# Seven products instead of plain sums for the second pair of weight chunks, in three of seven groups of an MLP, with block sums prepared during the attention part

## The chip, the cores and the metric

One core of a Trainium2 chip. The time is that of the program on the device in microseconds (us); the time before is the median of 3 runs. All engines of the core run their own instruction streams in order: TensorE (PE; its weight loads are listed as PEld), VectorE (DVE), ScalarE (ACT), GpSimd (POOL) and SyncE (SP), which here only issues DMAs. Differences of less than 0.2% (2.3 us) are not told apart.

## The reference

One decoder layer for 256 tokens of width 2048, in float32: three groups of mixers, an output projection, and an MLP of width 8192.

```python
def token_mixers(xn, ...):
    proj = jnp.einsum('bsd,de->bse', xn, w_in)
    # A: sparse attention; a small indexer scores all keys, the top 64 of each query are kept
    # B: mLSTM, chunkwise; C: differential attention
    ...
    return jnp.concatenate([y_a, y_m, y_c], axis=-1)

def reference(x, ...):
    mixed = token_mixers(x, ...)
    x = layer_norm(ALPHA * x + mixed @ w_out, ln1_g, ln1_b)
    h = jnp.square(jax.nn.relu(x @ w_up))
    return layer_norm(ALPHA * x + h @ w_down, ln2_g, ln2_b)
```

## The kernel before

**Splitting.** Every float32 operand of TensorE is used as a sum hi + lo of two rounded parts. A weight block [128 x 1024] comes as half of a 1 MB load (`load_raw`, L86, on SP's queue, three `raw` buffers), ScalarE casts it to hi (L90) and VectorE subtracts, lo = raw - hi (L91). Four buffers hold hi and four hold lo. TensorE needs three kinds of matmuls in a product, hi x hi, hi x lo and lo x hi.

**Units.** `unit_t` (L158, L159) computes 128 columns of a projection from one load of 1 MB: two halves of eight pairs of matmuls, 512 and 256 columns each. After each half `tick()` moves a clock on and runs work that was put off for so many ticks. `run_units` (L208 to L210) does the same for value projections. In mixer A the indexer's top 64 are found on VectorE by eight rounds of MAX8 and MATCH_REPLACE8 (L261, L262) on two blocks of queries, masked on GpSimd by AFFINE_SELECT (L264), between the splits of the units that run on TensorE meanwhile.

**MLP.** The hidden layer is cut into eight groups of eight units. While the units of group g + 1 are computed (`up`), group g is multiplied with its part of `w_down`, whose 2048 columns are four chunks of 512. Chunks 0 and 1 together are a matrix of 2 x 2 blocks and are done by the seven products of Strassen's scheme in Winograd's form (`product`, L884 to L886, 12 matmuls each): `pair_steps` makes the four needed sums of weight blocks on VectorE (L910 to L921, [128 x 2048] each) between the products. `make_blocks` and `make_sums` (L846, L853) prepare the same on the side of h in the tile `ms`, whose slices by form are `forms`. Chunks 2 and 3 are done plainly (`plain`, 48 matmuls each, L958 to L960). A string gives the order: U is a unit, a the next product of chunks 0 and 1, c and d the plain chunks. `out_block` and `macc` are where results add up; four of chunk pair 0's products stay in PSUM over all groups, the other three are added to `acc` by VectorE (L899). `pair_sums` joins the products at the end. A scheduler orders each engine's stream beforehand.

Of the kernel before, what the change touches and what calls it, by code (L numbers as in the profile page):

```python
# [11 lines left out]
F32 = mybir.dt.float32  # L12
# [12 lines left out]
FG = 8  # L25
FT = DFF // P // FG
TOPK = 64
ALPHA = 2.0 ** 0.25
EPS = 1e-5
LAM_INIT = 0.8 - 0.6 * math.exp(0.0)  # L30
# [12 lines left out]

def slopes(n):
    return [float(np.float32(2.0) ** np.float32(-8.0 * i / n)) for i in range(1, n + 1)]


@with_exitstack
def trunk_kernel(ctx: ExitStack, tc: tile.TileContext, xT, x, w_qi, w_t, w_va0, w_va, w_vm0, w_vm, w_vc,
# [21 lines left out]
    def tick():  # L71
        clock[0] += 1
        due = [f for d, f in queue if d <= clock[0]]
        queue[:] = [(d, f) for d, f in queue if d > clock[0]]
        for f in due:
            f()


    raws = [wp] * 3
# [22 lines left out]


    xs = fix.tile([P, KT, 2 * S], F32R, name="xs")
    ms = fix.tile([P, KT, 2 * S], F32R, name="ms")

    rx = fix.tile([P, 4240], F32, name="rx")

    ry = fix.tile([P, 4656], F32, name="ry")


    ones = mp.tile([P, P], F32, name="ones")
# [411 lines left out]
    for h in range(HM):  # L524
# [2 lines left out]
        m_head(h, q, k)  # L527
        conv_silu(13 + 2 * h, HM + h, k)


    sl_c = slopes(HC)
    sc_c = 64 ** -0.5
# [297 lines left out]

    A11, A12, A21, A22, S1, S2, S3, S4 = range(8)
    HT = FT // 2
    forms = ms.rearrange("p a b -> p (a b)").rearrange("p (f s k t) -> p f s k t", f=8, s=2, k=HT)

    macc = ry[:, 0:4 * 512].rearrange("p (i n) -> p i n", i=4)
    KEPT = {1: 0, 5: 1, 6: 2, 7: 3}
# [25 lines left out]
    def load_blocks(g, p):  # L862
        b11, b22, b21 = (fp.tile([P, 2048], F32, tag=n, name=n, bufs=1) for n in ("b11", "b22", "b21"))
        b12 = ry[:, 2048:4096]
        nc.sync.dma_start(b11, w_down[g, 2 * p, 0])
        nc.sync.dma_start(b12, w_down[g, 2 * p + 1, 0])
        nc.sync.dma_start(b22, w_down[g, 2 * p + 1, 1])
        nc.sync.dma_start(b21, w_down[g, 2 * p, 1])
        return b11, b12, b22, b21

    def product(g, p, i, f, b):

        if p == 0 and i in KEPT:
            if g == 0:
                kept[i] = mx("pk")
            ps, first, last = kept[i], g == 0, g == FG - 2
        else:
            ps, first, last = psb.tile([P, 512], F32, tag="big", name="pp"), True, True
        for q in range(2):
            hi, lo = split(b, 1024 * q, 1024 * q + 1024)  # L880
            for kk in range(2):
                k = 2 * q + kk
                w_hi, w_lo = hi[:, 512 * kk:512 * kk + 512], lo[:, 512 * kk:512 * kk + 512]
                nc.tensor.matmul(ps, forms[:, f, 0, k, :], w_hi, start=first and k == 0, stop=False)  # L884
                nc.tensor.matmul(ps, forms[:, f, 0, k, :], w_lo, start=False, stop=False)  # L885
                nc.tensor.matmul(ps, forms[:, f, 1, k, :], w_hi, start=False, stop=last and k == HT - 1)  # L886
        if p == 0 and i in KEPT:
            return
        if i in KEPT:
            a = macc[:, KEPT[i]]  # L890
            if g == 0:
                nc.scalar.copy(a, ps)
                return
        else:
            a = out_block(p, *((0, 0), (0, 1), (1, 0))[i - 2])
            if g == 0:
                nc.vector.scalar_tensor_tensor(a, a, ALPHA, ps, ALU.mult, ALU.add)
                return
        nc.vector.tensor_add(a, a, ps)  # L899

    def out_block(p, t, c):
        return acc[:, t, 1024 * p + 512 * c:1024 * p + 512 * c + 512]
# [1 line left out]
    def pair_steps(g, p, blocks):  # L904

        b11, b12, b22, b21 = blocks
        product(g, p, 1, A11, b11)
        yield
        product(g, p, 2, A12, b21)
        nc.vector.tensor_sub(b12, b12, b11)  # L910
        yield
        product(g, p, 3, S4, b22)
        nc.vector.tensor_sub(b22, b22, b12)
        yield
        product(g, p, 6, S2, b22)
        yield
        product(g, p, 5, S1, b12)
        nc.vector.tensor_sub(b11, b22, b11)
        yield
        product(g, p, 7, S3, b11)  # L920
        nc.vector.tensor_sub(b21, b21, b22)  # L921
        yield
        product(g, p, 4, A22, b21)
        yield

    def pair_sums(p):

        m = macc
        if p == 0:
            raw = wp.tile([P, 2048], F32, tag="raw", name="raw", bufs=3)  # L930
            m = raw.rearrange("p (i n) -> p i n", i=4)
            for i, j in KEPT.items():
                nc.scalar.copy(m[:, j], kept[i])
        p1, p5, p6, p7 = (m[:, j] for j in range(4))
        (c11, c12), (c21, c22) = ([out_block(p, t, c) for c in range(2)] for t in range(2))
        nc.vector.tensor_add(p6, p6, p1)
        nc.vector.tensor_add(p7, p7, p6)
        nc.vector.tensor_add(p6, p6, p5)
        nc.vector.tensor_add(p5, p5, p7)
        nc.vector.tensor_add(c11, c11, p1)  # L940
        nc.vector.tensor_add(c12, c12, p6)
        nc.vector.tensor_add(c21, c21, p7)
        nc.vector.scalar_tensor_tensor(c22, c22, ALPHA, p5, ALU.mult, ALU.add)

    def plain(g, c):

        pss = [psb.tile([P, 512], F32, tag="big", name="pst") for _ in range(2)]
        for i in range(2):
            raw = load_raw(w_down[g, c, i], 2048)
            for hf in range(2):  # L950
                hi, lo = split(raw, 1024 * hf, 1024 * hf + 1024)
                for kk in range(2):
                    k = 2 * hf + kk
                    w_hi, w_lo = hi[:, 512 * kk:512 * kk + 512], lo[:, 512 * kk:512 * kk + 512]
                    for t in range(2):
                        f = 2 * t + i
                        first, last = (i, k) == (0, 0), (i, k) == (1, HT - 1)
                        nc.tensor.matmul(pss[t], forms[:, f, 0, k, :], w_hi, start=first, stop=False)  # L958
                        nc.tensor.matmul(pss[t], forms[:, f, 0, k, :], w_lo, start=False, stop=False)  # L959
                        nc.tensor.matmul(pss[t], forms[:, f, 1, k, :], w_hi, start=False, stop=last)  # L960
        for t in range(2):
            a = acc[:, t, 512 * c:512 * c + 512]
            if g == 0:
                nc.vector.scalar_tensor_tensor(a, a, ALPHA, pss[t], ALU.mult, ALU.add)
            else:
                nc.vector.tensor_add(a, a, pss[t])

    def put_out(t, c, cs, a):
        (nc.sync if c % 2 else nc.scalar).dma_start(out[t, :, cs], a)
# [12 lines left out]
    hs[1] = fp.tile([P, FT, S], F32, name="h1")  # L982


    TURNS = "UUUaaaUcaaaUdUaUU"
    LAST = "UUUaaaUaUaUaUaUcd"
    for g in range(FG - 1):
        pairs = {"a": pair_steps(g, 0, load_blocks(g, 0))}
        units = iter(range(FT))
        for n, what in enumerate(TURNS if g < FG - 2 else LAST):  # L990
            if what == "U":
                up(g + 1, next(units))
            elif what in "cd":
                plain(g, "cd".index(what) + 2)
            else:
                next(pairs[what])
            if n == 0:
                make_blocks(g)
            elif n == 1:
                make_sums(g)  # L1000
    pair_sums(0)

    split_to(hs[1], xs[:, 0:FT, 0:S], xs[:, 0:FT, S:])
    gb = [h.rearrange("p a b -> p (a b)") for h in hs]
# [86 lines left out]
```

## Time and profile before

| | |
|---|---|
| median of 3 runs | 1172.65 us (1172.16 to 1172.98) |
| profiled execution | 1172.39 us, span from first to last instruction 1170.3 us |
| TensorE busy | 1156.0 us, 99% of the span |
| VectorE busy | 870.1 us, 74% |
| ScalarE busy | 639.4 us, 55% |
| GpSimd busy | 15.7 us, 1% |
| DMA | 226 MB, mean 193 GB/s |

The busy times are of one profiled execution, in which matmuls are drawn with their whole pipelined length: neighbours overlap, so what a matmul takes of TensorE's time is read from start to start. What lies around the span (1172.39 less 1170.3 us) is start and end of the program.

### The profile page before, as it was taken

How to read it: one execution, taken by the hardware profiler on the slowest of the kernel's cores; microseconds unless marked ns; L12 is line 12 of the kernel's file. 1: busy time of each engine (PE TensorE's matmuls, PEld its weight loads, DVE VectorE, ACT ScalarE, POOL GpSimd, SP SyncE). 2: the span in 40 equal slices, each digit the busy share in tenths (PEclk: the TensorE clock that was granted, in tenths of full speed). 3: DMA queues.
4: the chain of work that ended last, by engine and by line, in shares of the span. 5: the costliest groups of instructions: out<-in, count | busy, mean ns of one | idle time of the engine just before them, and what ended most of it. 6: DMA issues, size and time to landing. Idle time of an engine off the chain costs nothing.

```text
span 1170.3 us, 15441 instructions
## 1 busy us (share of the span) xinstructions
PE 1156.0 (99%) x6002; PEld 990.6 (85%) x6002; DVE 870.1 (74%) x1196; ACT 639.4 (55%) x917; POOL 15.7 (1%) x32
## 2 busy tenths in 40 slices
PE   8999999999999999999999999999999999999996
PEld 7898899988888888888888888888888888888885
DVE  5596556677776679679679679679679689688767
ACT  5545456544655452565475475475475475475541
POOL 1000000000000000000000000000000000000002
PEclk9999999999999999999999999999999999999999
DMA  9554446654754573655645645636636636644461
GB/s 326 190 195 166 147 163 209 230 174 166 277 204 166 180 255 139 240 193 185 232 159 192 237 146 206 231 140 216 227 134 222 232 122 235 231 145 139 159 242 72
DMA packets 34788, 225.98 MB, mean 193 GB/s; under 512 B 4118, under 2 KB 4508, under 8 KB 10908
## 3 DMA queue, kind: packets, MB, share of 16 engines
q1 hardware_dynamic: 33420, 217.67, 52.6%
q0 software_dynamic: 576, 4.19, 1.0%
q10 hardware_dynamic: 720, 3.15, 0.7%
q8 instruction: 47, 0.77, 0.3%
q14 instruction: 25, 0.20, 0.1%
HBM read 222.89 MB, written 2.11 MB: 192 GB/s over the span
## 4 chain that ended last, share of the span: by engine, by line
PE 93%; DVE 4%; issue 1%; ACT 1%; DMA 1%; SPq 0%; DVEq 0%
PE ps L158 28%; PE ps L159 15%; PE pst L208 6%; PE pst L210 6%; PE pst L209 6%; PE pst L960 4%; PE pst L959 4%; PE pst L958 4%; DVE lo L91 3%; PE psl L665 2%; PE psl L667 2%; PE psl L668 2%; PE pk L884 2%; PE pk L886 2%; PE pk L885 2%
## 5 line engine op out<-in xcount | busy, mean ns | idle before, releaser
L91 DVE TENSOR_TENSOR lo<-raw,hi 128x1024 fp32r<-128x1024 f32 (+5 forms) x352 | 417.8, 1192 | 216.0 <-ACT hi L90 215.2
L90 ACT CAST hi<-raw 128x1024 fp32r<-128x1024 f32 (+5 forms) x353 | 360.2, 1021 | 339.2 <-PE ps L158 150.0
L158 PE MATMUL ps<-xs,hi 128*128 128x512 f32 x1472 | 517.7, 393 | 0.0
L159 PE MATMUL ps<-xs,lo 128*128 128x256 f32 x1472 | 416.3, 283 | 1.2 <-DVE lo L91 1.1
L158 PEld LDWEIGHTS ps<-xs,hi 128*128 128x128 f32 x1472 | 276.5, 188 | 57.3 <-issue 0.3
L159 PEld LDWEIGHTS ps<-xs,lo 128*128 128x128 f32 x1472 | 278.8, 189 | 6.8 <-DVE lo L91 5.6
L90 ACT CAST hi<-b 128x1024 fp32r<-128x1024 f32 x84 | 88.3, 1052 | 58.2 <-PE pst L960 33.6
L91 DVE TENSOR_TENSOR lo<-b,hi 128x1024 fp32r<-128x1024 f32 x84 | 101.6, 1223 | 19.1 <-ACT hi L90 19.1
L959 PE MATMUL pst<-lo,ms 128*128 128x512 f32 x224 | 88.7, 396 | 0.0
L960 PE MATMUL pst<-hi,ms 128*128 128x512 f32 x224 | 88.6, 396 | 0.0
L958 PE MATMUL pst<-hi,ms 128*128 128x512 f32 x224 | 87.7, 396 | 0.0
L208 PE MATMUL pst<-hi,xs 128*128 128x384 f32 (+4 forms) x224 | 80.2, 358 | 0.0
L209 PE MATMUL pst<-lo,xs 128*128 128x384 f32 (+4 forms) x224 | 78.7, 351 | 0.0
L210 PE MATMUL pst<-hi,xs 128*128 128x384 f32 (+4 forms) x224 | 78.7, 351 | 0.0
L958 PEld LDWEIGHTS pst<-hi,ms 128*128 128x128 f32 x224 | 42.1, 188 | 10.0
L960 PEld LDWEIGHTS pst<-hi,ms 128*128 128x128 f32 x224 | 42.2, 188 | 9.8
L959 PEld LDWEIGHTS pst<-lo,ms 128*128 128x128 f32 x224 | 42.2, 188 | 9.8
L208 PEld LDWEIGHTS pst<-hi,xs 128*128 128x128 f32 x224 | 42.2, 189 | 3.1 <-issue 0.7
L884 PE MATMUL pk<-hi,ms 128*128 128x512 f32 x112 | 44.4, 397 | 0.0
L885 PE MATMUL pk<-lo,ms 128*128 128x512 f32 x112 | 44.3, 396 | 0.0
L886 PE MATMUL pk<-hi,ms 128*128 128x512 f32 x112 | 44.3, 396 | 0.0
L210 PEld LDWEIGHTS pst<-hi,xs 128*128 128x128 f32 x224 | 42.2, 189 | 2.0
(283 smaller groups left out, 1453.5 us busy)
## 6 DMA issues: line engine op xcount, KB each, us to landing
raw<-in_w_up_dram SPq DMA_DIRECT2D x64, 1024.0 KB, 4.9
raw<-in_w_t_dram SPq DMA_DIRECT2D x32, 1024.0 KB, 4.8
raw<-in_w_down_dram SPq DMA_DIRECT2D x28, 1024.0 KB, 4.9
b<-in_w_down_dram SPq DMA_DIRECT2D x21, 1024.0 KB, 4.9
raw<-in_w_oam_dram SPq DMA_DIRECT2D x12, 1024.0 KB, 4.9
raw<-in_w_vm_dram SPq DMA_DIRECT2D x12, 768.0 KB, 4.2
raw<-in_w_dnl_dram SPq DMA_DIRECT2D x8, 1024.0 KB, 6.3
ry<-in_w_down_dram SPq DMA_DIRECT2D x7, 1024.0 KB, 4.8
```

The lines of the kernel that those rows point to most:

```text
L90: nc.scalar.copy(hi, src)
L91: eng.tensor_sub(lo, src, hi.bitcast(F32))
L158: nc.tensor.matmul(ps, hi[:, P * kk:P * kk + P], xs[:, k, :], start=(k == 0), stop=False)
L159: nc.tensor.matmul(ps[:, 0:S], lo[:, P * kk:P * kk + P], xs[:, k, 0:S], start=False, stop=(k == KT - 1))
L208: nc.tensor.matmul(pss[t][:, :n], a_hi, w_hi, start=first, stop=False)
L209: nc.tensor.matmul(pss[t][:, :n], a_hi, w_lo, start=False, stop=False)
L210: nc.tensor.matmul(pss[t][:, :n], a_lo, w_hi, start=False, stop=last)
L884: nc.tensor.matmul(ps, forms[:, f, 0, k, :], w_hi, start=first and k == 0, stop=False)
L885: nc.tensor.matmul(ps, forms[:, f, 0, k, :], w_lo, start=False, stop=False)
L958: nc.tensor.matmul(pss[t], forms[:, f, 0, k, :], w_hi, start=first, stop=False)
L959: nc.tensor.matmul(pss[t], forms[:, f, 0, k, :], w_lo, start=False, stop=False)
L960: nc.tensor.matmul(pss[t], forms[:, f, 1, k, :], w_hi, start=False, stop=last)
```

## The change

In groups 0, 1 and 2 (`AHEAD`) chunks 2 and 3 are done by seven products as well. Their sums of weight blocks do not depend on the data, so they are made earlier: `block_sums` runs as a sequence of steps, one per `tick()` once the clock is beyond `START`, during the mixers. A job is a column slice of 512 of one group: four loads of 256 KB on GpSimd's queue (L146), four subtractions [128 x 512] on VectorE (L154), four stores to memory on GpSimd's queue (L157), behind which the loads of the job after next are issued. There are 12 jobs of seven steps. Their two rooms (`lent`) are the second half of the tile `ms`, which is not used until later; `ms` is therefore cut in two (`Halves`). `ready_steps` loads three raw blocks and the four stored sums on SP's queue and multiplies. The products of the second pair are put away by ScalarE into `new` and added to their place by an accumulating DMA on GpSimd's queue (L961, L962) in groups 1 and 2; in group 0 they are written directly. `pair_sums(1)` joins them during group 3.

```diff
+START = 8
+AHEAD = 3
...
     def tick():
...
+        if clock[0] > START:
+            next(blocks, None)
...
+    ms = Halves(KT // 2)
+    ms.parts.append(fix.tile([P, KT // 2, 2 * S], F32R, name="ms0"))
+    lent = fix.tile([P, KT // 2, 2 * S], F32, tag="ms1", name="lent", bufs=1)
...
+    def block_sums():
+        jobs = [(n // 4, slice(512 * (n % 4), 512 * (n % 4) + 512), [lent[:, 4 * (n % 2) + i, :] for i in range(4)])
+                for n in range(4 * AHEAD)]
+
+        def load(n):
+            for g, cs, room in jobs[n:n + 1]:
+                for r, (c, i) in zip(room, ((2, 0), (3, 0), (3, 1), (2, 1))):
+                    pin(nc.gpsimd.dma_start(r, w_down[g, c, i][:, cs]))
+
+        load(0)
+        load(1)
+        for _ in range(4):
+            yield
+        for n, (g, cs, (b11, b12, b22, b21)) in enumerate(jobs):
+            for d, x, y in ((b12, b12, b11), (b22, b22, b12), (b11, b22, b11), (b21, b21, b22)):
+                pin(nc.vector.tensor_sub(d, x, y))
+                yield
+            for i, b in enumerate((b12, b22, b11, b21)):
+                nc.gpsimd.dma_start(sums_d[g][i][:, cs], b)
+            load(n + 2)
+            for _ in range(3):
+                yield
...
-        nc.vector.tensor_add(a, a, ps)
+        if p == 0:
+            nc.vector.tensor_add(a, a, ps)
+        else:
+            d = fp.tile([P, 512], F32, tag="new", name="new", bufs=4)
+            nc.scalar.copy(d, ps)
+            nc.gpsimd.dma_start(a, d, accum_op=ALU.add)
...
+    def ready_steps(g):
+
+        for i, f, src in ((1, A11, w_down[g, 2, 0]), (2, A12, w_down[g, 2, 1]), (3, S4, w_down[g, 3, 1]),
+                          (6, S2, sums_d[g][1]), (5, S1, sums_d[g][0]), (7, S3, sums_d[g][2]),
+                          (4, A22, sums_d[g][3])):
+            product(g, 1, i, f, load_raw(src, 2048))
+            yield
...
+    second = pair_sums(1)
+    FIRST = "UUUababUabUababUabUabU"
     TURNS = "UUUaaaUcaaaUdUaUU"
     LAST = "UUUaaaUaUaUaUaUcd"
...
+        if g < AHEAD:
+            pairs["b"] = ready_steps(g)
...
+            elif n > 2 and g == AHEAD:
+                next(second, None)
```

Where the scheduler puts the first job is seen in the streams. VectorE in the selection of mixer A before, from the split of 776 columns on (MATCH_REPLACE and MAX are rounds of the selection, lo is a split for the units):

```order
L91 TENSOR_TENSOR lo<-raw,hi 128x776 [waits Activation_49]
L262 MATCH_REPLACE rx<-m_668,rx 128x256 [waits DVE_49]
L91 TENSOR_TENSOR lo<-raw,hi 128x1024 [waits DMAHW7_49,Activation_49]
L261 MAX m_671<-rx 128x8 [waits DVE_49]
L262 MATCH_REPLACE rx<-m_671,rx 128x256 [waits DVE_49]
L261 MAX m_674<-rx 128x8 [waits DVE_49]
L91 TENSOR_TENSOR lo<-raw,hi 128x1024 [waits Activation_49]
L262 MATCH_REPLACE rx<-m_674,rx 128x256 [waits DVE_49]
L261 MAX m_677<-rx 128x8 [waits DVE_49]
L91 TENSOR_TENSOR lo<-raw,hi 128x1024 [waits DMAHW0_49,Activation_49]
```

The same place of VectorE after the change, where `lent` stands for the first job's subtractions and DMASW for a wait for DMAs of GpSimd's queue:

```order
L314 MAX m_683<-rx 128x8 [waits DVE_49]
L315 MATCH_REPLACE rx<-m_683,rx 128x256 [waits DVE_49]
L314 MAX m_686<-rx 128x8 [waits DVE_49]
L154 TENSOR_TENSOR lent<-lent 128x512 [waits DMASW1_49,DMASW0_49]
L315 MATCH_REPLACE rx<-m_686,rx 128x256 [waits DVE_49]
L154 TENSOR_TENSOR lent<-lent 128x512 [waits DMASW2_49,DVE_49]
L314 MAX m_689<-rx 128x8 [waits DVE_49]
L154 TENSOR_TENSOR lent<-lent 128x512 [waits DVE_49]
L315 MATCH_REPLACE rx<-m_689,rx 128x256 [waits DVE_49]
L154 TENSOR_TENSOR lent<-lent 128x512 [waits DMASW3_49]
L314 MAX m_692<-rx 128x8 [waits DVE_49]
L109 TENSOR_TENSOR lo<-raw,hi 128x1024 [waits Activation_49]
```

The third lo split of these now stands behind the four subtractions and two more rounds.

GpSimd's stream around it, after the change (before, the two AFFINE_SELECT of L264 followed each other):

```order
L317 AFFINE_SELECT rx<-rx 128x128 [waits DVE_49]
L146 DMA lent<-in_w_down_dram 128x512 x8
L157 DMA sums_80<-lent 128x512 [waits DMASW0_49,DVE_49]
L157 DMA sums_80<-lent 128x512 [waits DMASW1_49,DVE_49]
L157 DMA sums_80<-lent 128x512 [waits DMASW2_49,DVE_49]
L157 DMA sums_80<-lent 128x512 [waits DMASW3_49,DVE_49]
L146 DMA lent<-in_w_down_dram 128x512 [waits DMASW4_49,DMASW2_49]
L146 DMA lent<-in_w_down_dram 128x512 [waits DMASW5_49,DMASW0_49]
L146 DMA lent<-in_w_down_dram 128x512 [waits DMASW6_49,DMASW1_49]
L146 DMA lent<-in_w_down_dram 128x512 [waits DMASW7_49,DMASW3_49]
L317 AFFINE_SELECT rx<-rx 128x256 [waits DVE_49]
```

The second AFFINE_SELECT has come to stand behind the first job's stores and the third job's loads.

VectorE in group 1 before, from the second product on (`b_` are weight blocks of chunks 0 and 1, raw a block loaded for units or plain chunks, L899 adds a product to its place):

```order
L91 TENSOR_TENSOR lo<-b_5470,hi 128x1024 [waits Activation_49] x2
L913 TENSOR_TENSOR b_5470<-b_5470,ry 128x2048 [waits DVE_49]
L899 TENSOR_TENSOR rx<-rx,pp 128x512 [waits PE_49]
L91 TENSOR_TENSOR lo<-raw,hi 128x1024 [waits DMAHW5_49,Activation_49]
L899 TENSOR_TENSOR rx<-rx,pp 128x512 [waits PE_49]
L91 TENSOR_TENSOR lo<-raw,hi 128x1024 [waits Activation_49]
L91 TENSOR_TENSOR lo<-raw,hi 128x1024 [waits DMAHW6_49,Activation_49]
L91 TENSOR_TENSOR lo<-raw,hi 128x1024 [waits Activation_49]
```

And after, from the third product of the first pair on (raw is here also a block of the second pair; L958 is the add that was L899, L976 and L981 were L913 and L918):

```order
L109 TENSOR_TENSOR lo<-b_5643,hi 128x1024 [waits Activation_49]
L109 TENSOR_TENSOR lo<-b_5643,hi 128x1024 [waits PE_49,Activation_49]
L976 TENSOR_TENSOR b_5643<-b_5643,ry 128x2048 [waits DVE_49]
L109 TENSOR_TENSOR lo<-raw,hi 128x1024 [waits DMAHW3_49,PE_49,Activation_49]
L981 TENSOR_TENSOR b_5642<-b_5643,b_5642 128x2048 [waits DVE_49]
L874 TENSOR_TENSOR half<-ps,half 128x256 [waits Activation_49]
L958 TENSOR_TENSOR rx<-rx,pp 128x512 [waits PE_49]
L109 TENSOR_TENSOR lo<-raw,hi 128x1024
L109 TENSOR_TENSOR lo<-raw,hi 128x1024 [waits DMAHW4_49,Activation_49]
L109 TENSOR_TENSOR lo<-raw,hi 128x1024 [waits Activation_49]
```

Two subtractions, a piece of a unit and an add now stand between the four splits of two products.

## Rows read from the trace of the kernel before

**Rows 1.** The page, part 1: busy us (share of the span) xinstructions.

```profile
PE 1156.0 (99%) x6002; PEld 990.6 (85%) x6002; DVE 870.1 (74%) x1196; ACT 639.4 (55%) x917; POOL 15.7 (1%) x32
```

**Rows 2.** The page, part 4: the chain that ended last, by engine.

```profile
PE 93%; DVE 4%; issue 1%; ACT 1%; DMA 1%; SPq 0%; DVEq 0%
```

**Rows 3.** Windows: length, busy us by engine, granted clock, DMA share, GB/s.

```profile
60.00:90.00 30.00, 30.00 (x175) 27.55 (x174) 26.61 (x70) 15.21 (x24) 1.09 (x3) 1.00 0.58 210
135.00:211.00 76.00, 76.00 (x442) 74.28 (x441) 44.88 (x89) 41.93 (x72) 0.00 (x0) 1.00 0.55 190
211.00:300.00 89.00, 89.00 (x513) 79.27 (x512) 66.97 (x130) 46.34 (x66) 0.00 (x0) 1.00 0.51 178
300.00:330.00 30.00, 30.00 (x162) 25.64 (x161) 20.04 (x43) 15.61 (x23) 1.24 (x2) 1.00 0.85 319
607.85:694.78 86.93, 86.76 (x437) 73.05 (x436) 68.09 (x68) 51.32 (x69) 0.00 (x0) 1.00 0.55 194
```

**Rows 4.** Timeline of PE at the first products of group 1: start us, us.

```profile
613.09 0.40 PE L884 MATMUL pp<-hi,ms 128*128 128x512 f32 x1
...
618.69 0.40 PE L158 MATMUL ps<-xs,hi 128*128 128x512 f32 x1
...
619.72 0.38 PE L159 MATMUL ps<-xs,lo 128*128 128x256 f32 x1 [0.17 <-DVE lo L91]
...
620.28 0.39 PE L158 MATMUL ps<-xs,hi 128*128 128x512 f32 x1
...
623.06 0.39 PE L158 MATMUL ps<-xs,hi 128*128 128x512 f32 x1
```

**Rows 5.** Timeline of VectorE there: start us, us (of all in a row, xcount).

```profile
617.85 0.68 DVE L899 TENSOR_TENSOR rx<-rx,pp 128x512 f32<-128x512 f32 x1
618.44 1.22 DVE L91 TENSOR_TENSOR lo<-raw,hi 128x1024 fp32r<-128x1024 f32 x1
...
620.17 4.63 DVE L91 TENSOR_TENSOR lo<-raw,hi 128x1024 fp32r<-128x1024 f32 x4
624.72 2.29 DVE L918 TENSOR_TENSOR b<-b,b 128x2048 f32<-128x2048 f32 x1
```

**Rows 6.** Waits of weight loads: us in total, times, longest us.

```profile
PEld ps L159 <- DVE lo L91: 5.6, 13, 0.7
```

**Rows 7.** Groups by line of ScalarE, 520 to 960 us: xcount | busy us, mean ns.

```profile
L90 ACT CAST hi<-raw 128x1024 fp32r<-128x1024 f32 x120 | 125.9, 1049 | 94.3 <-PE ps L158 75.4 <-PE pk L886 6.9 <-PE pst L960 6.8
...
L90 ACT CAST ms<-sum 128x512 fp32r<-128x512 f32 x20 | 12.2, 621 | 0.2
```

**Rows 8.** Timeline of VectorE in the selection of mixer A.

```profile
71.28 1.21 DVE L91 TENSOR_TENSOR lo<-raw,hi 128x1024 fp32r<-128x1024 f32 x1
72.40 0.08 DVE L262 MATCH_VALUE_LOAD rx<-m,rx 128x8 f32 x1
...
73.26 1.21 DVE L91 TENSOR_TENSOR lo<-raw,hi 128x1024 fp32r<-128x1024 f32 x1
```

**Rows 9.** Timeline of PE there.

```profile
74.62 0.28 PE L159 MATMUL ps<-xs,lo 128*128 128x256 f32 x1
```

**Rows 10.** Timeline of GpSimd.

```profile
67.37 0.29 POOL L264 TENSOR_SCALAR_AFFINE_SELECT rx<-rx 128x128 f32<-128x128 f32 x1 [1.31 <-DVE rx L263]
...
315.28 0.70 POOL L806 DMA_DIRECT2D ry<-in_g_dram  x1 [234.65 <-DVE ms L218]
```

**Rows 11.** DMA issues: xcount, KB each, us from issue to landing.

```profile
ry<-in_g_dram POOLq DMA_DIRECT2D x1, 1024.0 KB, 5.5
...
h<-in_b_dram POOLq DMA_DIRECT2D x1, 1024.0 KB, 8.8
...
out_dram<-rx SPq DMA_DIRECT2D x4, 256.0 KB, 2.1
...
gct<-in_gc_dram SPq DMA_DIRECT2D x1, 256.0 KB, 4.7
```

**Rows 12.** Timeline of VectorE beside the second of these.

```profile
315.44 2.35 DVE L91 TENSOR_TENSOR lo<-raw,hi 128x1024 fp32r<-128x1024 f32 x2
```

More of the change, by code (lines that the diff above doesn't have):

```diff
@@ L45, in slopes, with __init__, __getitem__ @@
     return [float(np.float32(2.0) ** np.float32(-8.0 * i / n)) for i in range(1, n + 1)]
+class Halves:
+    def __init__(self, n, parts=()):
+        self.n, self.parts = n, list(parts)
+    def __getitem__(self, key):
+        k = key[1]
+        if isinstance(k, int):
+            return self.parts[k // self.n][(key[0], k % self.n, *key[2:])]
+        part = k.start // self.n
+        return self.parts[part][(key[0], slice(k.start - part * self.n, k.stop - part * self.n), *key[2:])]
 @with_exitstack
@@ L104, in trunk_kernel @@
     xs = fix.tile([P, KT, 2 * S], F32R, name="xs")
-    ms = fix.tile([P, KT, 2 * S], F32R, name="ms")
+    ms = Halves(KT // 2)
+    ms.parts.append(fix.tile([P, KT // 2, 2 * S], F32R, name="ms0"))
+    lent = fix.tile([P, KT // 2, 2 * S], F32, tag="ms1", name="lent", bufs=1)
     rx = fix.tile([P, 4240], F32, name="rx")
     ry = fix.tile([P, 4656], F32, name="ry")
+    sums_d = [dram.tile([4, P, 2048], F32, name=f"sums{g}") for g in range(AHEAD)]
+    pin = tc.keep_in_program_order
+    def block_sums():
[18 more added lines that the diff above has]
+                yield
+    blocks = block_sums()
     ones = mp.tile([P, P], F32, name="ones")
@@ L528, in trunk_kernel @@
         conv_silu(13 + 2 * h, HM + h, k)
+    for _ in blocks:
+        pass
+    ms.parts.append(fix.tile([P, KT // 2, 2 * S], F32R, tag="ms1", name="ms1", bufs=1))
     sl_c = slopes(HC)
@@ L832, in trunk_kernel @@
     HT = FT // 2
-    forms = ms.rearrange("p a b -> p (a b)").rearrange("p (f s k t) -> p f s k t", f=8, s=2, k=HT)
+    forms = Halves(4, [a.rearrange("p a b -> p (a b)").rearrange("p (f s k t) -> p f s k t", f=4, s=2, k=HT)
+                       for a in ms.parts])
     macc = ry[:, 0:4 * 512].rearrange("p (i n) -> p i n", i=4)
@@ L937, in pair_sums @@
         nc.vector.tensor_add(p7, p7, p6)
+        yield
         nc.vector.tensor_add(p6, p6, p5)
         nc.vector.tensor_add(p5, p5, p7)
+        yield
         nc.vector.tensor_add(c11, c11, p1)
         nc.vector.tensor_add(c12, c12, p6)
+        yield
         nc.vector.tensor_add(c21, c21, p7)
         nc.vector.scalar_tensor_tensor(c22, c22, ALPHA, p5, ALU.mult, ALU.add)
+        yield
     def plain(g, c):
@@ L962, in plain @@
             a = acc[:, t, 512 * c:512 * c + 512]
[L963 to L966, printed above, removed]
+            nc.vector.tensor_add(a, a, pss[t])
     def put_out(t, c, cs, a):
@@ L988, in trunk_kernel @@
         pairs = {"a": pair_steps(g, 0, load_blocks(g, 0))}
+        if g < AHEAD:
+            pairs["b"] = ready_steps(g)
         units = iter(range(FT))
-        for n, what in enumerate(TURNS if g < FG - 2 else LAST):
+        for n, what in enumerate(FIRST if g < AHEAD else TURNS if g < FG - 2 else LAST):
             if what == "U":
@@ L1000, in trunk_kernel @@
                 make_sums(g)
-    pair_sums(0)
+            elif n > 2 and g == AHEAD:
+                next(second, None)
+    for _ in pair_sums(0):
+        pass
     split_to(hs[1], xs[:, 0:FT, 0:S], xs[:, 0:FT, S:])
```

## The prediction

> **What bounds the kernel now.** I read the totals first: TensorE is busy 1156.0 of 1170.3 us, VectorE 870.1, ScalarE 639.4, GpSimd 15.7 [rows 1]. The chain that ended last lies on TensorE for 93% [rows 2]. So the time is TensorE's work plus the moments in which it waits. Next the windows by stage, at granted clock 1.00 (the 2.4 GHz level) in every one [rows 3]: TensorE is full in all of them. What differs is the second engine. VectorE is at 26.61 of 30 us while the top-64 selection of mixer A runs (60 to 90), at 44.88 of 76 in mixer B's value passes, 66.97 of 89 in its heads, 68.09 of 86.93 in a down group.
>
> A matmul's row overlaps its neighbours, so I take start to start: 24 matmuls of two products run from 613.09 to the next unit's first at 618.69, 0.2333 us each; eight pairs of a unit take 623.06 - 620.28 = 2.78 us [rows 4]. So a product of 12 matmuls is 2.80 us and its half 1.40, half a unit 2.78. VectorE's pitches in the same way [rows 5]: a lo split (624.72 - 620.17) / 4 = 1.14, a [128x512] add 618.44 - 617.85 = 0.59; a [128x2048] subtraction lasts 2.29.
>
> TensorE loses little now: waits for a lo split are 5.6 us in 13 pieces, longest 0.7 [rows 6]. One shows the pattern: the lo that ends at 618.44 + 1.22 = 619.66 stands behind an eviction add on VectorE [rows 5], and TensorE takes it at 619.72 after 0.17 idle [rows 4].
>
> **The change, term by term.** Sums are made against the profiled execution's 1172.39 us (span 1170.3 and 2.09 around it); the median, 1172.65, lies 0.26 above.
>
> *Matmuls removed.* A group's chunks 2 and 3 take 7 products of 12 matmuls for 96 plain ones, so 12 fewer, 36 in three groups. 36 x 0.2333 = 8.40 us, all on the path, since TensorE is the bound on either side of them. This is the sure term.
>
> *VectorE in the groups.* Six more half splits a group (28 for products and 16 for units, where 14, 16 and 8 stood): 6 x 1.14 = 6.8 us. Four plain eviction adds go (2.4 us); in groups 1 and 2 the second pair's evictions are ScalarE copies and accumulating DMAs, so nothing comes back. 68.09 + 4.4 = 72.5 of about 84 us: not a bound on the mean. ScalarE gets 6 hi casts of 1.05 and, in groups 1 and 2, seven PSUM copies of [128x512], for which the nearest row is the cast of that size, 0.62 [rows 7]: 51.32 + 6.3 + 4.3 = 62 of 84 us. SP loads three more blocks of 1 MB a group, and the accumulates read and write up to 4 MB: (16.9 + 3 + 4) MB / 84 us = 285 GB/s, where a window before shows 319 [rows 3]. Splitting the tile ms in two changes addresses only.
>
> *Waits in the groups.* The order has one tight spot: after product a3's splits come a [128x2048] subtraction, one lo of b3, another such subtraction, an add that evicts a3, then b3's second lo. The eviction cannot begin before TensorE ends a3, which is when it begins b3. So b3's second lo ends 0.59 + 1.22 + about 0.06 = 1.87 us after that, and TensorE wants it after 1.40: it waits at least 0.47. If the two subtractions also eat the lead (2.29 x 2 + two splits, against 2.8 of TensorE), 0.8. Before, a group lost 5.6 / 7 = 0.8 in such spots; the first, behind the block sums of h, stays. I add 0.3 a group, **0.9** in three (bounds 0 and 2.4).
>
> *The first job's four subtractions.* These I expect to be seen. Before, the lo begun at 71.28 ends at 72.49 [rows 8] and TensorE uses it at 74.62 [rows 9], 2.1 us later. Now four [128x512] subtractions, two MATCH_REPLACE and two MAX stand ahead of it: 4 x 0.59 = 2.4, and twice from 72.40 to 73.26 [rows 8], 1.7 (1.6 if the subtractions hide the gap between the two). It ends at 72.49 + 4.1 = 76.6, TensorE waits **2.0 us** from 74.62. To it comes w, the wait of the first subtraction for its loads. They are issued on GpSimd's queue behind the AFFINE_SELECT that ends at 67.66; an issue takes 0.70 at most in the rows [rows 10], the second load, for which the subtraction waits, leaves at about 68.9. A 256 KB transfer lands 2.1 us (a store on SP's queue) or 4.7 us (gct) after its issue, a 1 MB one of GpSimd's 8.8 at most [rows 11]. VectorE has done what stands ahead of the first subtraction at 71.28, as before: w is 0 by the first, 2.3 by the second, 6.4 by the third. By size the first two are nearest; I take 0.3. The later splits follow each 2.0 us against 2.78 of TensorE, so they catch up; nothing adds.
>
> *The other 44 subtractions.* 44 x 0.59 = 26 us of VectorE between 80 and 300 us, where it has 31 us free of 76 in the passes and 22 of 89 in the heads [rows 3]. They stand one at a time between splits. I cost them at nothing; what hides them is that free time and the lead of the splits over TensorE (2.1 us at the split of 71.28). Where the lead is gone, one costs 0.59; if that were so for five of them: bound 3.
>
> *GpSimd's queue.* The second block's AFFINE_SELECT, on which the masking of mixer A waits, now stands behind four stores and four loads that wait for these stores. Job 0's last subtraction ends near 75.3; issue, landing of 2.1 to 4.7 and four issues put it at 81 to 82.5, when VectorE, itself 2.4 us later than before, has the input ready. The lo queued behind that wait has the lead named above, some 2 us. Nothing; if landings take 8.8, up to 2.
>
> *Accumulating DMAs.* The adds that join the products in group 3's stretch wait for the last accumulate; copy 0.6, issue 0.7, landing 2.1 to 8.8 against two products, 5.6 us, that stand between the last product of the second pair and these adds in the order: I take 0, bound 5 (8.8 + 1.3 less 5.6). No row of before has an accumulating DMA.
>
> *Sum.* 1172.39 - 8.40 + 0.9 + 2.0 + 0.3 = 1167.2; with 0.26 to the median, **1167.4 us**.
>
> **Rivals.** (1) *The first loads land late* (w of 3 or more). Of GpSimd's four issues before, one, at 315.28, took 0.70 beside two VectorE splits that began at 315.44 and took 2.35 for two, as always [rows 10, 12]. That speaks against VectorE and GpSimd's issues slowing each other. For it: its 1 MB landings reach 8.8. With w = 5: 1172. Not to be told from before.
> The Trainium skill, SBUF — State Buffer, section "SBUF: two separate sides", warns that a DMA from GpSimd's queue waits for its descriptors while VectorE is in a two-port mode ("DVE blocks DMA"). By that rule the loads of the first job would wait out the splits ahead of the first subtraction, and this rival would hold; the issue at 315.28 and its landing in 5.5 us for 1 MB [rows 10, 11] do not show such a wait.
>
> (2) *The groups give back more.* With products in alternating pairs the lead of the splits is shorter, since a half of a product lasts 1.40 us and a split's hi and lo 1.05 and 1.22 one behind the other. If each of a group's seven pairs costs 0.3 to 0.5 instead of one spot, 2 to 3.5 us a group: 6 to 10 in all. VectorE's 72.5 of 84 speaks against more than the half of it. 1170.
>
> (3) *Slower: the DMA engines in the value passes.* From 135 to 211 us they move 190 GB/s, 14.4 MB [rows 3]. About five and a quarter jobs fall in there, each 1 MB in and 1 MB out (1.05 million bytes): 11.1 MB, together 25.5 MB, 336 GB/s. The most a window shows is 319 at a busy share of 0.85 [rows 3]. If 319 is the top, the pass needs 80 us and the loads are 4 us late: 1171. It turns the sign at 25.5 MB / (76 + 5.2) = 314 GB/s and gives 1175 below 25.5 MB / 83.6 us = 305. For it: the figure is higher than any seen. Against: 0.85 is not full, and 319 / 0.85 = 375 would hold it.
>
> (4) *No wait at the first job.* If VectorE had the subtractions done in gaps that the rows do not show: 1165. VectorE is at 26.61 of 30 there [rows 3], and the rows around 71 us follow each other without a gap [rows 8], so little speaks for it.
>
> **Numbers.** Forecast (its own range 1165 to 1169.5) 0.58; (1) 0.13, half of it under 1170.3; (2) 0.13, two thirds of it under; (3) 0.10, a fifth of it under 1175; (4) 0.06. A measurement of this kernel tells 0.2%, 2.35 us, from no change. Faster, below 1170.3: 0.58 + 0.065 + 0.085 + 0.06 = 0.79; slower, above 1175: 0.08 of rival 3; the same: the remaining 0.13. The range goes from 1164.2, the fourth rival with small waits in the groups, to 1172.0, the first with w = 5; what it leaves out is the far end of (1), nearly all of (3) and half of (4), some 0.15.
>
> **What would show it.** Right: a product's matmuls at 0.233 and a group from start to start near 84.2 us in groups 0 to 2, 86.9 after; one idle of TensorE of about 2 us near 75 us, ended by a lo split; a second-lo wait near 0.5 us in the pairs. Wrong: a stall at the first job over 4 us, ended by a subtraction that waited for a DMA (rival 1); waits for lo splits of more than 2 us a group (2); TensorE waiting between 130 and 215 us with the DMA share at 0.9 (3); idle of VectorE before the adds of the products' join, ended by an accumulating DMA.

## The result

The changed kernel takes 1182.5 us (median of 4 runs, 1182.1 to 1186.4) against 1172.6: ratio 1.0092, 95% interval 1.0071 to 1.0114. It is slower by 0.9%, where 1167.4 was predicted. Its profiled execution took 1182.09 us with a span of 1180.4, 10.1 more than before.

The totals on the page of the changed kernel (part 1, then the granted clock in 40 slices from part 2) hardly differ from [rows 1]: TensorE's busy time is the same although it has 36 matmuls fewer.

```profile
PE 1156.2 (98%) x5966; PEld 988.4 (84%) x5966; DVE 913.9 (77%) x1261; ACT 667.2 (57%) x955; POOL 80.4 (7%) x142
...
PEclk9989999999999999999999999989999999999998
```

The clock has two dips, in the third and the 27th slice (the last slice is the program's end). Waits of the changed kernel, in us in total, times, longest:

```profile
PEld ps L212 <- DVE lo L109: 14.6, 13, 5.2
...
DVE lent L154 <- DMA lent<-in_w_down_dram: 5.4, 2, 3.2
...
DVE rx L1016 <- DMA rx<-new: 3.7, 1, 3.7
...
DVE ry L1007 <- DMA ry<-new: 2.2, 1, 2.2
...
DVE ry L1008 <- DMA ry<-new: 1.3, 1, 1.3
```

TensorE's waits for lo splits have gone from 5.6 to 14.6 us, and the longest from 0.7 to 5.2 ([rows 6]); VectorE has new waits for DMAs. Windows of the changed kernel (length, busy us of PE, PEld, DVE, ACT, POOL, granted clock, DMA share, GB/s), around the first job, in the value passes, and from the first product of one group to that of the next, for groups 1 to 3:

```profile
60.00:74.00 14.00, 14.00 (x82) 13.26 (x81) 11.50 (x39) 7.85 (x12) 5.08 (x10) 1.00 0.54 182
74.00:80.00 6.00, 1.11 (x8) 0.71 (x6) 5.16 (x13) 1.05 (x1) 2.17 (x4) 0.85 1.01 396
80.00:85.00 5.00, 5.00 (x16) 4.32 (x17) 4.80 (x8) 0.12 (x1) 2.13 (x4) 0.50 0.89 280
135.00:211.00 76.00, 76.00 (x443) 73.38 (x442) 54.74 (x112) 38.81 (x70) 19.32 (x36) 1.00 0.82 285
614.83:699.20 84.37, 83.97 (x425) 70.72 (x424) 72.35 (x70) 60.60 (x82) 5.97 (x7) 1.00 0.78 259
699.20:784.45 85.25, 84.35 (x425) 70.46 (x423) 72.18 (x71) 56.27 (x74) 5.96 (x7) 1.00 0.78 256
784.45:878.60 94.15, 89.70 (x437) 75.28 (x437) 72.77 (x75) 55.44 (x77) 0.00 (x0) 0.96 0.51 179
```

Groups 1 and 2 take 84.4 and 85.3 us where a group took 86.9, as forecast. The loss is elsewhere. The first product of group 0 begins at 533.6 us where it began at 523.3: 10.4 us are lost before the MLP. The four group lengths of 0 to 3 are 81.2, 84.4, 85.3 and 94.2, in sum 345.0, where they were 84.4, 86.9, 86.9 and 86.9, in sum 345.2: what three groups gained the fourth gave back. 10.4 - 0.2 is the 10.1 of the span, within rounding. Of the 10.4, 7.2 are lost at the first job, as shown next. Of the rest 2.6 are lost between 213 and 228 us: set one by one against the same matmuls before, TensorE's run 7.7 us late from 85 to 213 us, and 10.3 at 228. Shortly before, VectorE waits for a load of a later job, and then for the rows of mixer B's gates, which SP's queue brings as a broadcast:

```profile
199.11 0.69 DVE L154 TENSOR_TENSOR lent<-lent 128x512 f32<-128x512 f32 x1 [2.26 <-DMA lent<-in_w_down_dram]
204.94 0.56 DVE L477 SCALAR_TENSOR_TENSOR rx<-rx,negm 128x384 f32<-128x384 f32 x1 [2.48 <-DMA rx<-rows]
```

**First place, the first job.** VectorE and then TensorE of the changed kernel, in order of time (start us, us):

```profile
71.25 0.43 DVE L314 MAX8 m<-rx 128x8 f32<-128x256 f32 x1
74.84 0.69 DVE L154 TENSOR_TENSOR lent<-lent 128x512 f32<-128x512 f32 x1 [3.17 <-DMA lent<-in_w_down_dram]
...
75.86 0.69 DVE L154 TENSOR_TENSOR lent<-lent 128x512 f32<-128x512 f32 x1
...
78.73 1.21 DVE L109 TENSOR_TENSOR lo<-raw,hi 128x1024 fp32r<-128x1024 f32 x1
```

```profile
74.71 0.39 PE L211 MATMUL ps<-xs,hi 128*128 128x512 f32 x1
79.99 0.58 PE L212 MATMUL ps<-xs,lo 128*128 128x256 f32 x1 [4.89 <-DVE lo L109]
80.37 0.63 PE L211 MATMUL ps<-xs,hi 128*128 128x512 f32 x1
...
84.85 0.49 PE L211 MATMUL ps<-xs,hi 128*128 128x512 f32 x1
...
85.30 0.39 PE L211 MATMUL ps<-xs,hi 128*128 128x512 f32 x1
```

VectorE stands 3.17 us before the first subtraction, waiting for its load. The split behind it ends at 79.94, TensorE takes it at 79.99 and has lost 79.99 - 74.71 - 0.23 = 5.05 us. Then seven pairs of matmuls from 80.37 to 84.85 take 4.48 us where they take 2.43 at full clock ([rows 4]: 2.78 for eight): the window 80 to 85 shows a granted clock of 0.50, the 1.2 GHz level, and costs another 2.1 us. From 84.85 on it is 2.4 GHz again.

Why the load was late stands in the DMA view of the changed kernel between 69 and 75 us (packets, MB, share of the 16 engines; then issues with KB and us to landing):

```profile
q1 hardware_dynamic: 144, 1.05, 46.9%
q0 software_dynamic: 246, 0.84, 45.4%
...
lent<-in_w_down_dram POOLq DMA_DIRECT2D x7, 256.0 KB, 7.1
raw<-in_w_t_dram SPq DMA_DIRECT2D x1, 1024.0 KB, 6.4
```

GpSimd's queue (q0) had the engines for 45% and SP's (q1) for 47%: a raw load of 1 MB ran at the same time and moved 1.05 MB while `lent` got 0.84. The first load landed 4.0 us after its issue; the second, for which the subtraction waits, took 6.1 us and landed at 74.75, and the raw load landed at 75.2. GpSimd's queue moved 0.27 MB from 69 to 71.7 us, while VectorE was busy for 2.61 of 2.7 us, and 0.26 MB from 71.7 to 74, while VectorE stood idle: this is sharing, not a queue that VectorE holds up. It agrees with the Trainium skill, DMA: Bandwidth & Descriptors, section "Issuing engines are not separate DMA queues", that DMAs interleave on the same 16 engines whichever engine started them. The wait that the Trainium skill, SBUF — State Buffer, section "SBUF: two separate sides", names for VectorE's two-port modes, weighed in rival 1, does not show in these rows; rival 1 took the splits to run in such a mode, which no row shows.

**Second place, the joining adds.** The end of the second pair's last product on TensorE, its copy on ScalarE and its accumulate on GpSimd, then VectorE and TensorE of the changed kernel:

```profile
764.44 0.40 PE L944 MATMUL pp<-hi,ms 128*128 128x512 f32 x1
766.23 0.58 ACT L961 COPY new<-pp 128x512 f32<-128x512 f32 x1
767.11 0.85 POOL L962 DMA_DIRECT2D rx<-new  x1 [12.43 <-ACT new L961]
```

```profile
769.34 0.69 DVE L1014 TENSOR_TENSOR rx<-rx,ry 128x512 f32<-128x512 f32 x1
773.75 0.69 DVE L1016 TENSOR_TENSOR rx<-rx,ry 128x512 f32<-128x512 f32 x1 [3.73 <-DMA rx<-new]
774.36 1.22 DVE L109 TENSOR_TENSOR lo<-raw,hi 128x1024 fp32r<-128x1024 f32 x1
...
787.97 1.22 DVE L109 TENSOR_TENSOR lo<-raw,hi 128x1024 fp32r<-128x1024 f32 x1
```

```profile
784.45 0.50 PE L942 MATMUL pk<-hi,ms 128*128 128x512 f32 x1
789.24 0.58 PE L212 MATMUL ps<-xs,lo 128*128 128x256 f32 x1 [4.28 <-DVE lo L109]
789.62 0.63 PE L211 MATMUL ps<-xs,hi 128*128 128x512 f32 x1
...
794.10 0.63 PE L943 MATMUL pk<-lo,ms 128*128 128x512 f32 x1
```

The last accumulate is issued at 767.1 and lands 6.6 us later; VectorE stands 3.73 us in front of the add that needs it, with splits and the block sums of h queued behind. They come late at the next tight spot, the one behind the block sums: TensorE stops from 784.45 to 789.24 (4.6 us), and seven pairs at half clock follow again (2.1 us, and 0.4 for two matmuls of the product).

### The profile page after: what moved, and what is told of

It reads as the page before. It is cut to its first block, busy times and chain, and to the rows that moved or that the text cites. A ratio compares the mean times of both kernels' runs of the same rounds, so it can differ in the third digit from the quotient of the medians.

```text
span 1180.4 us, 15757 instructions
## 1 busy us (share of the span) xinstructions
PE 1156.2 (98%) x5966; PEld 988.4 (84%) x5966; DVE 913.9 (77%) x1261; ACT 667.2 (57%) x955; POOL 80.4 (7%) x142
## 4 chain that ended last, share of the span: by engine, by line
PE 71%; issue 16%; DVE 7%; DMA 3%; ACT 1%; POOL 1%; DVEq 0%; POOLq 0%; ACTq 0%; SPq 0%
PE ps L211 24%; PE ps L212 13%; DVE lo L109 3%; PE pst L263 3%; PE pst L261 3%; PE pst L262 3%; PE pst L1035 3%; PE pst L1034 3%; PE pst L1033 2%; PE psl L722 2%; PE psl L724 2%; PE psl L725 2%; PE pk L942 1%; PE pk L944 1%; PE pk L943 1%
## 5 line engine op out<-in xcount | busy, mean ns | idle before, releaser
L109 DVE TENSOR_TENSOR lo<-raw,hi 128x1024 fp32r<-128x1024 f32 (+5 forms) x370 | 437.4, 1190 | 177.2 <-ACT hi L108 176.1
L108 ACT CAST hi<-raw 128x1024 fp32r<-128x1024 f32 (+5 forms) x371 | 377.8, 1023 | 340.7 <-PE ps L211 151.3
L212 PE MATMUL ps<-xs,lo 128*128 128x256 f32 x1472 | 418.2, 284 | 10.5 <-DVE lo L109 10.4
L212 PEld LDWEIGHTS ps<-xs,lo 128*128 128x128 f32 x1472 | 280.3, 190 | 16.0 <-DVE lo L109 14.6
L943 PE MATMUL pp<-lo,ms 128*128 128x512 f32 x168 | 66.8, 398 | 1.3 <-DVE lo L109 1.3
L944 PE MATMUL pp<-hi,ms 128*128 128x512 f32 x168 | 66.5, 396 | 0.0
L942 PE MATMUL pp<-hi,ms 128*128 128x512 f32 x168 | 66.4, 396 | 0.0
L1034 PE MATMUL pst<-lo,ms 128*128 128x512 f32 x128 | 50.6, 395 | 0.0
L1035 PE MATMUL pst<-hi,ms 128*128 128x512 f32 x128 | 50.6, 395 | 0.0
L1033 PE MATMUL pst<-hi,ms 128*128 128x512 f32 x128 | 50.1, 395 | 0.0
L261 PEld LDWEIGHTS pst<-hi,xs 128*128 128x128 f32 x224 | 42.2, 188 | 3.5 <-issue 0.7
L262 PEld LDWEIGHTS pst<-lo,xs 128*128 128x128 f32 x224 | 42.1, 188 | 3.0 <-DVE lo L109 1.2
```

What stands on the lines that cost most here:

```text
L108: nc.scalar.copy(hi, src)
L109: eng.tensor_sub(lo, src, hi.bitcast(F32))
L212: nc.tensor.matmul(ps[:, 0:S], lo[:, P * kk:P * kk + P], xs[:, k, 0:S], start=False, stop=(k == KT - 1))
L261: nc.tensor.matmul(pss[t][:, :n], a_hi, w_hi, start=first, stop=False)
L262: nc.tensor.matmul(pss[t][:, :n], a_hi, w_lo, start=False, stop=False)
```

## Experiments

All are compared on the same chip with the kernel before, 1172.6 to 1173.0 us. Where an edit is said to leave something out, the time is that of the work that is left.

**1. The first job later, alone.**

```diff
-START = 8
+START = 20
```

> START 20 instead of 8: the first job begins when the selection is over. Theory: of the changed kernel's 1182.5 us, 5.3 us are TensorE's stop at the first job (71 to 80 us) and 2.2 us the half clock that follows it to 84.9; both go, nothing takes their place: 1175 (1174 to 1176.5), granted clock 1.00 between 60 and 110 us. Rival (the jobs cost wherever they stand, because VectorE or the DMA engines are full there): the stop comes back at the next job, 1180 to 1183.

1174.5 us (1170.7 to 1177.1), 8.0 less than the changed kernel. The stop at 75 us and the half clock are gone (60 to 85 us all at 1.00), and no other came in their place before 200 us. The stop near 775 us stays, 4.31 us, with its dip of the clock. The theory holds.

**2. No accumulating DMAs, alone.**

```diff
-        if p == 0:
-            nc.vector.tensor_add(a, a, ps)
-        else:
-            d = fp.tile([P, 512], F32, tag="new", name="new", bufs=4)
-            nc.scalar.copy(d, ps)
-            nc.gpsimd.dma_start(a, d, accum_op=ALU.add)
+        nc.vector.tensor_add(a, a, ps)
```

> The second pair's products are added by VectorE from PSUM, as the first pair's are; no accumulating DMA. Theory: the 4.8 us stop of TensorE near 785 us and the half clock behind it (2.3 us) come from VectorE's waits for the accumulates (2.2, 1.3 and 3.7 us) before the joining adds; they go: 1175.5 (1174.5 to 1177). Rival (the stop is VectorE's own load, eight adds and the block sums of h in one place): 14 more adds of 0.59 us make it worse or leave it, 1182 to 1185.

1173.9 us (1172.4 to 1177.9), 8.7 less. No stop at the join, though the joining adds still stand ahead of the block sums of h (the last of them ends at 771.0 us, the block sums begin at 772.8). 14 more adds on VectorE cost nothing there, so its load was not the cause.

**3. Both edits.**

> The edits of the two runs before together. Theory: the two places are independent and no third one of their size exists: 1168 (1167 to 1170), faster than before the change by 0.2 to 0.5%. Rival (the products themselves do not gain, the groups give their 2.8 us back): 1172 or more, a group of the first three near 86.5 us.

1165.6 us (1164.7 to 1167.7), ratio to before 0.994, interval 0.9925 to 0.9955: 0.6% faster than before, and better than expected by 2.4, below the range as well. The two places are independent (8.0 + 8.7 = 16.7, and 16.9 was found). Windows of this version, the value passes and groups 1 to 3:

```profile
135.00:211.00 76.00, 74.58 (x428) 71.60 (x427) 52.35 (x104) 41.12 (x70) 20.38 (x38) 1.00 0.83 295
607.33:691.06 83.73, 83.73 (x426) 70.73 (x424) 75.84 (x77) 57.39 (x75) 0.00 (x0) 1.00 0.66 239
691.06:778.14 87.08, 86.76 (x440) 72.97 (x439) 83.65 (x88) 58.33 (x75) 0.00 (x0) 1.00 0.65 235
778.14:862.52 84.38, 84.14 (x423) 70.80 (x422) 65.26 (x65) 50.45 (x68) 0.00 (x0) 1.00 0.55 194
```

The group lengths 0 to 3 are 81.2, 83.7, 87.1 and 84.4, in sum 336.4: 8.8 less than before. (In this version 22.7 us lie between the last product of group 2 and the first of group 3, where 19.9 lie between the groups before: 2.8 us, the time of half a unit, have moved from group 3's window into group 2's.) The first product begins 2.9 us later than before. In the value passes TensorE is busy 74.58 of 76 us: VectorE waits 4.7 us for the broadcast of the gate rows, which lands 11.9 us after its issue where it took 8.0. The issue is late too: it waits for a small write of these rows, and from the issue of that write to the landing of the broadcast it is 17.1 us where it was 9.7.

**4. Fewer loads at once.** The second job's loads are issued behind the first job's subtractions.

```diff
         load(0)
-        load(1)
 ...
+            if n == 0:
+                load(1)
```

> As the changed kernel, but the second job's loads are issued behind the first job's subtractions and not with the first's, so 1 MB and not 2 MB stands on GpSimd's queue when the first subtraction waits. Theory (the 16 DMA engines are shared: from 74 to 80 us they are at a share of 1.0): the first job's loads land about 2 us earlier, TensorE's stop is about 3 us, and the whole 1178 to 1180; if the clock then stays at 1.00, 1177. Rival (GpSimd's queue itself is slow, whatever else is under way): the second load lands 6.3 us after its issue as now, the stop stays near 5 us, 1182 to 1183.

1181.8 us (1180.4 to 1183.7): the rival's number. VectorE waits 4.29 us, and TensorE's stop is 6.6, longer than before the edit. My theory of the burst falls: what stands behind the first loads on their queue doesn't hold them. But the rival's reason isn't shown by this either, since the queue shares the engines with a raw load here too: from 70 to 76.5 us GpSimd's queue had 45% of the engines and moved 0.97 MB, SP's 43% and 1.03 MB. The trace of experiment 3 speaks against a slow queue. The same second load of the first job, issued there at 81.58 us with the same loads ahead of it and behind it, has nothing of SP's beside it. Its row follows that of the changed kernel's second load (us from issue to landing last); then come the two queues and the engines of experiment 3 from its issue to its landing:

```profile
lent<-in_w_down_dram POOLq DMA_DIRECT2D x1, 256.0 KB, 6.1
lent<-in_w_down_dram POOLq DMA_DIRECT2D x1, 256.0 KB, 3.1
...
q0 software_dynamic: 195, 0.66, 69.7%
q1 hardware_dynamic: 8, 0.00, 0.1%
...
81.58:84.68 3.10, 3.10 (x20) 2.75 (x19) 3.04 (x4) 1.32 (x2) 3.10 (x6) 1.00 0.70 213
```

It lands in 3.1 us, with VectorE busy for 3.04 of them; the changed kernel's took 6.1 us beside 1.05 MB of SP's queue, and this experiment's 7.2 beside 1.02 MB. So neither GpSimd's queue by itself nor a full VectorE makes the load late; the landing goes with the raw load. No run moves the raw load alone.

**5. The last adds later.** With START 20; the accumulating DMAs stay. In it group 3's plain chunk 3 is added before the last join scales that block, so the output is another.

```diff
-            elif n > 2 and g == AHEAD:
+            elif n > 8 and g == AHEAD:
```

> START 20, and the eight adds that join the second pair's products begin later in group 3 (n > 8 for n > 2); the accumulating DMAs stay. It differs from the run with START 20 alone (1174.5 us) in the place of the last adds. Theory: an accumulate costs only where VectorE waits for its landing with splits queued behind; the last two waits (1.5 and 3.9 us) go, TensorE's 4.3 us stop near 775 us and the half clock go: 1168 (1166.5 to 1170). Rival (the accumulates and ScalarE's copies cost by themselves, in transfers and ScalarE's time): 1173 or more.

1167.6 us (1166.3 to 1169.2), 6.9 below experiment 1, as expected, and TensorE has no stop. But only the last of the three waits is gone: VectorE still waits 2.8 and 0.9 us for the first two accumulates, with splits behind them, and group 2, in which they lie, takes 84.4 us like group 1. So a wait for an accumulate costs by where it stands; here it was the one shortly ahead of the block sums of h. The 2.0 us that remain to experiment 3 are less than is told apart; in the traces the four groups are 0.7 us longer (337.0 and 336.4).

**6. No jobs.** No block sums at all, VectorE adds as in experiment 2; the products take raw blocks.

> No jobs beside the mixers at all; the products take raw blocks in place of the sums (the block sums are left out, so the second pair's result is another), and VectorE adds the second pair's products. Theory: what is left is the 36 matmuls (-8.4 us) and 0.2 to 0.3 us of waits a group: 1164.8 less nothing, and the jobs of the version with both edits (1165.6) cost 1 to 2.5 us, in the place where the broadcast of the gate rows lands 11.9 us after its issue: 1163 to 1165. Rival (the jobs cost nothing beside the mixers): 1165.6; rival (the groups give back more): 1167 or more.

1163.6 us (1163.1 to 1163.8). This is what the 36 matmuls give: 9.0 us less than before, with an interval of 7.5 to 10.9 around their 8.4. The trace is finer: the four groups take 336.2 us where they took 345.2, 9.0 less. By the medians the jobs of experiment 3 cost 2.0 us, less than is told apart, though each of its runs is slower than each of these; in the traces its first product begins 2.9 us later than before, and here 0.4. Its runs lie 3 us apart where these lie within 0.7: the jobs bring the scatter as well.

**7. The first loads earlier.**

```diff
-START = 8
+START = 3
...
-        for _ in range(4):
+        for _ in range(9):
```

> As the changed kernel, with the first two jobs' loads five ticks earlier (START 3, nine steps of waiting for four): the scheduler then puts the first four subtractions into the selection's first half, with their loads landed. Theory: the 5.3 us stop was 3.2 us of waiting for a load and about 2 us of VectorE's own added work; the first part goes, and with a stop of 2 us or less the half clock does not follow: 1176 to 1178. Rival (VectorE's fullness alone makes the stop): 1181 or more.

1177.4 us (1177.2 to 1179.3), as expected, but in part by luck: the theory left 2 us of the stop in place, and they are gone, while 4.2 us that it did not foresee are lost at the kernel's start. TensorE has no stop and a clock of 1.00 from 60 to 95 us, though VectorE is busy 5.93 of 6 us between 74 and 80. The subtractions stand some earlier in the selection than before the edit, so it does not price them at the old place; it does show that a full VectorE alone makes no stop of 5 us. It loses elsewhere: group 0's first product begins 5.1 us later than before, 4.2 of it in the first 25 us, where the early loads now meet the kernel's first ones (the weight loads of the first units wait 8.0 us for hi and lo, 1.7 in the changed kernel, and from 10 to 30 us the DMA engines are full at 394 GB/s). The stop at the join stays, 4.31 us.

**8. A pause around the gate rows.** Both edits of experiment 3.

```diff
-        if clock[0] > START:
+        if clock[0] > START and not 57 <= clock[0] < 63:
...
-            for _ in range(3):
+            for _ in range(2 if clock[0] > 62 else 3):
```

> Both edits (START 20, VectorE adds), and no job step in six ticks around the broadcast of the gate rows; later jobs take six steps for seven. Theory: the rows land some 9 us and not 11.9 us after their issue, VectorE's wait of 4.7 us before the first of them and TensorE's 2.5 us near 200 to 210 go: 1163.5 (1162.5 to 1164.8) for 1165.6. Rival (the waits there come from the raw loads alone): 1165.6.

1165.5 us (1163.9 to 1166.5), not to be told from 1165.6. In the profiled run (1163.9) the rows land after 9.5 us, VectorE waits 2.3, and TensorE is busy 30.00 of 30 us from 185 to 215, where it was 28.59 without the pause. So the wait at the rows is real, and with the pause it costs TensorE nothing: the first product begins 0.4 us later than before the change, where it was 2.9 in experiment 3. That the median stays says that single runs lose their 2 us in other ways, which the one profile doesn't show.

**9. Jobs without subtractions.** Both edits; the stored blocks are raw.

> The version with both edits (1165.6 us) without the 48 subtractions: loads and stores stay, the stored blocks are raw, so the second pair's result is another. Theory: the 2.0 us by which that version stands above the one without jobs (1163.6) come from the transfers (the broadcast of the gate rows lands late), not from VectorE: 1165 to 1166, VectorE still waits 3 us or more for the rows, and single runs still lie 2 to 3 us apart. Rival (VectorE's 28 us of subtractions cost it): 1163.5 to 1164, runs within 1 us.

1164.3 us (1163.9 to 1166.0): between the two theories, with an interval (0.9914 to 0.9944) that overlaps those of 3 and 6. VectorE's wait for the rows is 4.6 us here too, though the broadcast lands 8.9 us after its issue. It is the small write ahead of it that is late: SP's queue waits for it 3.5 us here, 0.2 before the change (us in total, times, longest; before, then here):

```profile
SPq L417 <- DMA rows<-ra: 0.2, 1, 0.2
SPq L469 <- DMA rows<-ra: 3.5, 1, 3.5
```

From the write's issue to the landing it is 14.0 us, so transfers alone make that wait. How the 2 us divide between transfers and subtractions stays open.

**10. Four groups.** Both edits, AHEAD 4, five steps a job.

> The version with both edits, for four groups instead of three (AHEAD 4), jobs of five steps for seven so that 16 jobs fit. Theory: one more group saves 2.9 us; 16 jobs in the place of 12 load and store a third more in the same time, which costs 0 to 3 us: 1162.5 to 1165.5. Rival (the transfers are at their limit in the value passes): 1167 or more, with the granted clock falling after a stop there.

1181.2 us (1178.4 to 1181.8): the rival. Row of VectorE near 200 us (start us, us), and the window around TensorE's stop:

```profile
205.71 0.69 DVE L154 TENSOR_TENSOR lent<-lent 128x512 f32<-128x512 f32 x1 [11.29 <-DMA lent<-in_w_down_dram]
```

```profile
198.00:210.00 12.00, 3.40 (x16) 3.08 (x15) 4.09 (x7) 0.96 (x2) 3.03 (x7) 0.68 0.85 309
```

VectorE waits 11.29 us for a load; TensorE is busy 3.40 of 12 us, the DMA engines 85% at 309 GB/s. With a job every five ticks the transfers fall behind in the value passes. The fourth group and the shorter jobs were not tried apart.

## Why the prediction was wrong

Two of the signs of being wrong that the prediction names are in the rows: a stall at the first job over 4 us, ended by a subtraction that waited for a DMA, and idle of VectorE before the adds of the join, ended by an accumulating DMA. To the second step below belong two rows that I could have read beforehand. They are of the kernel before and show what SP's queue (q1) moved while a load of 1 MB on GpSimd's queue was under way (packets, MB, share of the engines), first for the one that landed in 5.5 us, then for the one that took 8.8 [rows 11]:

```profile
q1 hardware_dynamic: 44, 0.36, 17.9%
...
q1 hardware_dynamic: 290, 2.09, 61.0%
```

- **Matmuls removed, and waits in the groups.** Right in the main: 84.4 us for group 1 against the 84.2 foretold. (By the prediction's own terms, 86.93 - 2.80 + 0.3, it is 84.4; and group 0, foretold at 84.2 too, took 84.4 before the change and 81.2 after.) The waits were priced too high: I added 0.9 us in three groups; in the traces without accumulates the four groups are 8.8 to 9.0 us shorter (experiments 3 and 6), so they lose 0.4 to 0.6 less than before, not 0.9 more.
- **The first job's subtractions.** This step failed in w: "By size the first two are nearest; I take 0.3". It was 3.2. I read the landings by size and didn't look at what SP's queue moves at that moment. The trace of before had it, in the rows above: of two loads of one size the one with six times as much beside it took 8.8 us for 5.5. The 2.1 us that I took were those of a store, and the 4.7 of gct had 1.0 MB of other loads of SP's queue beside it. The size was inside my bounds (6.4), but I put it into a rival with 0.13. The 2.0 us of VectorE's own work is borne out by subtraction: 5.05 of stop less 3.17 of wait is 1.9.
- **What a stop costs.** No step had it: after the stops of 5.05 and 4.6 us TensorE ran at a granted clock of 0.50 for 4.9 and 5.7 us, which cost 2.1 and 2.5 us. Of this no run of before could tell, since its longest wait for a split was 0.7 us.
- **Accumulating DMAs.** This step failed as well: "I take 0", and it was 4.6 us of stop and 2.5 of half clock. The slack was nearly what I took: the product ends at 764.84 and VectorE is at the add at 770.03, 5.2 us for my 5.6. The landing, 6.6 us, was in my range, and with it my own sum, 6.6 + 1.3 - 5.6, is a wait of 2.3 us and not of 0. The rest of the measured 3.73 is mostly ScalarE, which begins the copy only 1.4 us after the product's end, behind a cast. Bound 5 would have held the stop alone.
- **The other subtractions and rival 3.** Taken at nothing; of the 10.4 us lost before the MLP, 3.2 are not the first job's, 2.6 of these near the gate rows, and experiment 3 has 2.9 of this kind. My 336 GB/s was too much (285 in the window of 76 us, into which the loads of four jobs fall and not of five and a quarter), but the mechanism was that of rival 3: a transfer on which VectorE waits lands late. That it would be the broadcast of the gate rows, no step had. Experiment 10 shows where it decides.
- **GpSimd's queue.** Right: the AFFINE_SELECT behind stores and loads cost nothing seen (VectorE waits 0.51 us for it, 0.50 before).

The sum with measured sizes: 1172.4 - 9.0 + 7.2 (first job) + 7.1 (join) + 3.2 (the other jobs) = 1180.9, against 1182.1 profiled. The rest, 1.2, is 1.7 us in the groups (345.0 in sum, less the join's 7.1, against the 336.2 of experiment 6), less 0.4 by which the program's start and end around the span are shorter. Groups 1 and 2 have it: group 1 is 84.4 us in the changed kernel and in experiment 5, which have accumulates, and 83.7 in experiments 3 and 6, with VectorE's adds. Which part of the accumulates makes it wasn't tried singly.

## What to carry to other kernels

Before an engine that feeds the bound one is made to wait for a transfer, look at what the other queues move at that moment, and price the landing by their sharing, not by a transfer that ran alone; then give it that much time, since everything queued behind waits with it. Side work that is free on the average pays at single spots: start it only when its data have landed (experiment 7), or place it after the stretch in which its engine is full (experiment 1). A stop of the bound engine of several us is to be priced with the half clock that follows.

## What was not expected of the hardware

After TensorE had stood still for 4.3 to 8.6 us it ran at a granted clock of 0.50 for 2.9 to 5.7 us (eight stops in six kernels; 2.9 us after the one of 6.6); after one of 2.6 us in experiment 10, one of 1.6 us in experiment 4, and after waits of up to 0.9, it was at 1.00. Two queues shared the DMA engines at 45 and 47% of their time from 69 to 75 us. An accumulating DMA's issue held GpSimd for 0.84 to 0.90 us, a plain store's for 0.54 at the median, and the accumulates of 256 KB landed 3.3 to 8.9 us after their issue.
